# A two-layer trunk kernel: attention slots dealt out by ScalarE and VectorE load, evictions and splits queued in a given order, gated states of the recurrence copied a slot later

## The chip, the cores and the metric

The kernel runs on one core of a Trainium2 chip. A core has TensorE (PE in the profile; its weight loads are PEld), VectorE (DVE), ScalarE (ACT), GpSimd (POOL) and SyncE (SP), which here issues the loads and stores. The metric is the device time of one execution in microseconds (us), the median of several.

## The reference

One sequence of 1024 positions, width 1024, all float32:

```python
# layer 0: two groups of 8 heads of 64
proj = h @ w_in                      # a_q, a_k, a_v, b_q, b_k, b_v, f_logit, gate
# A: window of 128, 2 key/value heads, learned bias and a sink per head
# B: causal, logits + F_t - F_s, F = cumsum(log_sigmoid(f_logit + b_f))
y = concat(a_out, b_out) * silu(gate)
x = x + gate(c) * (y @ w_out)
# layer 1: recurrent block
xr, gate = split(h @ w_in)
xc = conv4(xr)                       # causal, depthwise
r, i = sigmoid(xc @ w_a + b_a), sigmoid(xc @ w_x + b_x)   # in 8 diagonal blocks
hs_t = a_t * hs_(t-1) + sqrt(1 - a_t^2) * (i * xc)_t,  a = exp(-8 softplus(lam) r)
x = x + gate(c) * ((hs * silu(gate)) @ w_out)
# RMSNorm with a scale and a shift that depend on c before each mixer; a last RMSNorm
```

## The kernel before, in words

The state lies transposed, width on the 128 partitions in 8 tiles, positions along the free axis in two halves of 512. A float32 operand is split in two parts: a rounded high part (names ending in hi or h), and the difference, the low part (lo, l). A product is then three matmuls: high x high, low weight x high, high weight x low. Writing the high part is a copy on ScalarE, the low part a subtraction on VectorE or GpSimd that needs the copy. Weights come from HBM into one of three `raw` buffers (256 KB each) and are split there, in two halves of four 128-row blocks, into `whi` and `wlo` (four buffers each). All instructions pass through helpers, so every row of the profile shows line 85, and the tiles' names tell the place.

By time in the profile: up to 133 us the modulation, the first norm and the gate projection; 133 to 530 attention, interleaved with the projections of q, k and v and the first part of the output projection; to 590 the rest of that projection (`o0c`) and the first tiles of the recurrent block's input projection (`lx`); to 780 the recurrence; then the last output projection (`ps_o`), in three column blocks, and the last norm.

**Attention.** A unit is one head (B) or one pair (A) and a pair j of 128-query blocks. It has steps: S (scores into `sA`/`sB`, added to the bias by VectorE, exponential on ScalarE into `pA`/`pB`), T (`turn`: transpositions of the probabilities on TensorE into `ptA`/`ptB`, then `split_t` into `pth` and `ptl`), V (`product`: `oA`/`oB` from `pth`, then from `ptl`) and E (`rbT`, the scaling of the result). For B with j = 3 there are four key-block pairs, `ptB_<head>_3_0` to `_3_3`. A slot holds the steps of neighbouring units that are issued together. `weave` walks through the slots and puts projection matmuls (`ps_fill`) between the steps; they come from the generator `fill`, job by job, and `weave` gives each slot as many as level its PE cost with the others'. A job ends with its eviction (`use_q`, `use_k`, `use_v`, for the output projection `residual` and `split_act`), at once after the last matmul. The next job's weights are loaded and split when a job starts. `drip` holds a few further copies, one per eight fill matmuls, `late` one more, the transposition of v.

TensorE's order in attention is that of the program, since `pe` is in the set `ordered`. The other engines' instructions are placed by the scheduler, by its own times; `paced(name)` adds an engine to the set for some instructions. In the start and the recurrence every engine is in program order.

**Recurrence.** `slot(c)` works on one tile c of eight: 24 matmuls for each half of the input tile c + 2 (`ps_lx`), the gates (`psr`, `psi`), 24 for each half of the gate path (`ps_lg`). ScalarE takes r_r and i_r (sigmoids), then tanh, exp, square and root; VectorE runs the convolution and the scan `hs`. The gated state is made in three steps: `gate_s` (sigmoid of `ps_lg` on ScalarE and the product on VectorE), `gate_a` (times `hs`, on GpSimd), `gate_b` (copy to y1h on ScalarE, y1l on GpSimd). `split_next` splits the next weights in line and loads the ones after. `last_slot` (c = 7) also splits the first tiles of the last output projection with `split_out`; `AHEAD` of these tiles run seven of their eight blocks before TensorE needs the last state.

Of the kernel before, what the change touches and what calls it, by code (L numbers as in the profile page):

```python
# [22 lines left out]
AHEAD = 3  # L23
# [25 lines left out]
def hybrid_trunk(  # L49
# [635 lines left out]
    def use_q(q, name):  # L685


        def use(h, ps):
            o = slice(h * HALF, (h + 1) * HALF)
            for hd, (a, b) in enumerate(((0, 64), (64, 0))):  # L690
                copy(q[hd][a : a + 64, o], ps[a : a + 64], scale=-0.125)
                dve.scalar_tensor_tensor(
                    out=q[hd][b : b + 64, o], in0=ps[a : a + 64], scalar=-0.125,
                    in1=r32(q[hd][a : a + 64, o]), op0=ALU.mult, op1=ALU.subtract,
                )

        return use

    def use_k(kh, kl):
        def use(h, ps):  # L700
            o = slice(h * HALF, (h + 1) * HALF)
            for hd, (a, b) in enumerate(((0, 64), (64, 0))):
# [7 lines left out]
                gp.tensor_copy(kl[hd][b : b + 64, o], r32(lo))  # L710

# [51 lines left out]
    def unit_a(p, j, q, kh, kl, out):  # L763
# [65 lines left out]
        def end():  # L829
# [4 lines left out]
            "S": [(0.43, lambda r=r: score(r)) for r in two],  # L834
            "T": [(0.43, lambda r=r: turn(r)) for r in two],
            "V": [(0.43, lambda r=r: product(r)) for r in two],
            "E": [(0.22, end)],
# [10 lines left out]
    def unit_b(p, hd, j, src, out):  # L848
# [61 lines left out]
        def end():  # L910
            finish(out()[0], box["rb"], 4 + p, j, f"B_{p}_{j}")

        return {
            "S": [
                (2 * max(b - a, 128) / 2400, lambda r=r, i=i: score(r, i))
                for r in range(2) for i, (a, b, _) in enumerate(pieces(2 * j + r))
            ],
            "T": [(0.43, lambda m=m: turn(m)) for m in range(j + 1)],
            "V": [(0.43, lambda m=m: product(m)) for m in range(j + 1)],
            "E": [(0.22, end)] if hd else [],  # L920
# [3 lines left out]
    def use_v(v, name):  # L924
        def use(h, ps):
            t = at.tile([P, HALF], F32, tag="tv", name=f"vt_{name}_{h}", bufs=1)
            copy(t, ps)

            def later():
                pt = ps_t(f"vT_{name}_{h}")  # L930
                for i in range(4):
                    tp(pt[:, i * P : (i + 1) * P], t[:, i * P : (i + 1) * P])
                for hd in range(2):
                    src = pt.rearrange("p (t h d) -> p t h d", t=4, h=2)[:, :, hd]
                    o = v[:, 4 * h : 4 * h + 4, hd]
                    copy(o[:, :, 0:64], src)
                    sub(dve, o[:, :, 64:128], src, r32(o[:, :, 0:64]))

            return later
# [5 lines left out]
    late, drip = [], collections.deque()  # L945

    def fill(jobs, ahead=lambda: None):

        jobs = list(jobs)
        ws = {0: jobs[0][0]()}  # L950
        for n, (_, ks, xs, use) in enumerate(jobs):
            if n + 1 < len(jobs):
                ws[n + 1] = jobs[n + 1][0]()
            else:
                ahead()
            w = ws.pop(n)
# [31 lines left out]
    def job(ti, name, use):  # L988
        return (lazy(lambda: load_tile(wt[ti], name)), range(KT), both, use)
# [70 lines left out]
    def weave(slots, gen, total, first=0):  # L1060


        cost = [sum(c for c, _ in s) for s in slots]
        left = total - sum(next(gen) for _ in range(first))
        for i, slot in enumerate(slots):
            rest = sorted(cost[i:])

            level, acc = 0.0, 0.0
            for n, c in enumerate(rest):
                level = (left + acc + c) / (n + 1)  # L1070
                acc += c
                if n + 1 == len(rest) or level <= rest[n + 1]:
                    break
            give = max(level - cost[i], 0.0)
            left -= give
            part = give / max(len(slot), 1)
            for _, f in slot:
# [17 lines left out]

    for n, _ in enumerate(fill(jobs[0], jobs[1][0][0])):
# [29 lines left out]
    def then_split(jq, jv, jk):  # L1126
# [4 lines left out]
        def use_and_split(h, ps):  # L1131
            use(h, ps)
# [533 lines left out]
```

## Time and profile before

| what | value |
|---|---|
| median of 3 executions | 888.19 us (884.86 to 888.86) |
| profiled execution | 888.44 us, span 886.7 us, granted clock 0.986 |
| PE busy | 860.7 us (97%) |
| DVE, ACT, POOL busy | 564.5 (64%), 535.7 (60%), 378.1 us (43%) |
| attention, 133 to 530 us | PE 388.93 of 397.00 us |
| a slot of the recurrence | 25.5 to 25.9 us, PE 24.95 to 25.90 us |

A PE duration runs until the modelled end of a matmul, and consecutive matmuls overlap in it; the distance from start to start tells the pace. In brackets behind a row stands the idle time of its engine before it and what ended it. A row of waits says which engine's work waited for which other, the sum, how often, and the longest. A row of a window gives its length and then the busy time of each engine in it.

### The profile page before, as it was taken

The page shows a single profiled execution, that of the slowest core. Times are in us where ns is not written, and L with a number is a line of the kernel's source. Part 1 is how long each engine was busy: PE and PEld are TensorE (multiplying, and loading weights), DVE is VectorE, ACT ScalarE, POOL GpSimd, SP SyncE. Part 2 cuts the span into 40 slices and gives each one's busy share as a digit, 9 for nine tenths or more (in the row PEclk, how much of TensorE's full clock was granted, in tenths as well). Part 3 has the DMA queues.
Part 4 walks back from the last instruction along what each step waited for, and adds up shares of the span by engine and source line. Part 5 has one row for each costly group of instructions (what it writes and reads, how often), then busy time and mean ns, then how long its engine had stood idle before and what let it go on. Part 6 is the DMA issues. An engine that isn't in the chain of part 4 may idle for free.

```text
span 886.7 us, 13483 instructions
## 1 busy us (share of the span) xinstructions
PE 860.7 (97%) x4618; PEld 730.7 (82%) x4618; DVE 564.5 (64%) x1136; ACT 535.7 (60%) x1047; POOL 378.1 (43%) x427
## 2 busy tenths in 40 slices
PE   9999999999989999999999999999899999999995
PEld 8887898888878888888777888878688877878995
DVE  7886657688676565565656668276556666583453
ACT  5765124788676666566656647358666667774432
POOL 4843322343342232331744656532565555475100
PEclk9999999999999999999999999999899999999998
DMA  9944772100013322322373564421212212126042
GB/s 344 404 185 127 216 229 60 49 25 20 30 53 111 107 80 101 123 87 78 110 240 104 184 209 145 145 79 44 78 54 72 77 57 67 56 71 226 7 149 83
DMA packets 54620, 103.83 MB, mean 117 GB/s; under 512 B 6960, under 2 KB 20720, under 8 KB 54040
## 3 DMA queue, kind: packets, MB, share of 16 engines
q1 hardware_dynamic: 53400, 101.93, 34.8%
q10 hardware_dynamic: 1152, 1.05, 0.5%
q8 instruction: 36, 0.59, 0.3%
q14 instruction: 32, 0.26, 0.1%
HBM read 94.02 MB, written 8.93 MB: 116 GB/s over the span
## 4 chain that ended last, share of the span: by engine, by line
PE 66%; ACT 11%; DVE 10%; DMA 5%; POOL 4%; issue 3%; SPq 0%; DVEq 0%; POOLq 0%; ACTq 0%
PE ps_fill L85 22%; PE ps_o L85 10%; PE pst L85 5%; PE ps_o0c L85 5%; PE oB L85 4%; PE sB L85 4%; PE ptB L85 3%; DVE xc_r L85 3%; PE ps_v L85 3%; DVE hs_r L85 2%; DMA ada<-in_ada_dram 2%; PE ps_lx L85 2%; POOL sg_r L85 2%; PE sA L85 2%; PE ps_lg L85 2%
## 5 line engine op out<-in xcount | busy, mean ns | idle before, releaser
L85 PE MATMUL ps_o<-y1h,wo 128*128 128x256 f32 (+1 forms) x336 | 76.8, 323 | 2.2 <-DVE wo L85 1.1
L85 DVE TENSOR_TENSOR ptl_B<-ptB,pth_B 128x512 fp32r<-128x512 f32 (+1 forms) x80 | 50.8, 636 | 36.8 <-ACT pth_B L85 36.3
L85 ACT ACTIVATE pth_B<-ptB 128x512 fp32r<-128x512 f32 (+1 forms) x80 | 44.0, 551 | 44.6 <-PE ptB L85 43.7
L85 ACT ACTIVATE pB<-pB,mnB 128x128 f32<-128x128 f32 (+3 forms) x64 | 49.5, 774 | 31.3 <-DVE mnB L85 25.9
L85 PEld LDWEIGHTS ps_o<-y1h,wo 128*128 128x128 f32 x336 | 56.7, 192 | 7.5 <-ACT wo L85 1.5
L85 POOL TENSOR_SCALAR_AFFINE_SELECT pB<-pB 128x128 f32<-128x128 f32 x64 | 18.8, 296 | 96.3 <-DMA pB<-gd 71.6
L85 PE MATMUL pst<-hh,ws 128*128 128x512 f32 x192 | 55.3, 396 | 0.1
L85 PE MATMUL ps_o<-y1l,wo 128*128 128x256 f32 (+1 forms) x168 | 54.2, 323 | 0.0
L85 PE MATMUL ps_lg<-h1h,wlo_lg 128*128 128x512 f32 x128 | 51.3, 401 | 2.3 <-POOL wlo_lg L85 2.3
L85 PE MATMUL ps_lg<-h1h,whi_lg 128*128 128x512 f32 x128 | 51.4, 401 | 1.9 <-ACT whi_lg L85 1.9
L85 DVE SCALAR_TENSOR_TENSOR xc_r<-ps_lx,col,xc_r 128x509 f32<-128x509 f32 (+2 forms) x48 | 35.7, 745 | 24.6 <-ACT xt_r L85 23.5
L85 PE MATMUL ps_lg<-h1l,whi_lg 128*128 128x512 f32 x128 | 50.8, 397 | 0.0
L85 PE MATMUL ps_lx<-h1l,whi_lx 128*128 128x512 f32 x128 | 50.3, 393 | 0.2 <-POOL h1l L85 0.2
L85 PE MATMUL ps_lx<-h1h,whi_lx 128*128 128x512 f32 x128 | 50.3, 393 | 0.0
L85 PE MATMUL ps_lx<-h1h,wlo_lx 128*128 128x512 f32 x128 | 50.1, 391 | 0.0
L85 DVE CUSTOM_DVE_ANT_0 pB<-sB,pB 128x384 f32<-128x384 f32 (+2 forms) x64 | 35.4, 554 | 19.4 <-PE sB L85 9.3
L85 ACT ACT_TABLE_LOAD x35 | 44.9, 1283 | 3.6 <-issue 1.9
L85 PE MATMUL ptB<-ident,pB 128*128 128x128 f32 x288 | 45.1, 273 | 1.2 <-DVE ptl_B L85 0.7
L85 PEld LDWEIGHTS ptB<-ident,pB 128*128 128x128 f32 x288 | 35.8, 140 | 12.2 <-PE rbT_B L85 1.5
L85 POOL TENSOR_TENSOR wlo_lx<-raw_lx,whi_lx 128x512 fp32r<-128x512 f32 x16 | 30.6, 1929 | 32.0 <-ACT whi_lx L85 30.1
L85 PEld LDWEIGHTS pst<-hh,ws 128*128 128x128 f32 x192 | 35.9, 188 | 9.0 <-DVE mod L85 0.6
L85 ACT ACTIVATE sq_o<-x 128x512 f32<-128x512 f32 (+1 forms) x33 | 18.0, 545 | 33.3 <-DVE x L85 33.1
(313 smaller groups left out, 2838.7 us busy)
## 6 DMA issues: line engine op xcount, KB each, us to landing
ada<-in_ada_dram SPq DMA_DIRECT2D x32, 512.0 KB
x<-in_xT_dram SPq DMA_DIRECT2D x20, 256.0 KB
ada<-in_ada_dram SPq DMA_DIRECT2D x4, 1024.0 KB
pB<-gd SPq DMA_DIRECT2D x8, 512.0 KB
raw_o0a<-in_wo_dram SPq DMA_DIRECT2D x16, 256.0 KB
raw_o0c<-in_wo_dram SPq DMA_DIRECT2D x16, 256.0 KB
x1d<-x SPq DMA_DIRECT2D x16, 256.0 KB
raw_lx<-in_wl_dram SPq DMA_DIRECT2D x16, 256.0 KB
```

The source lines that it names most:

```text
L85: ins = issue(*args, **kw)
```

## The change

- In attention, `split_t` keeps its two instructions in program order on ScalarE and VectorE. Evictions are no longer issued at the end of a job, but as a list of pieces put at the front of `drip`; one piece is taken every four fill matmuls, in program order on both engines. What is left is issued at the end of a `fill`. `late` is gone; the transposition and split of v are pieces of it too.
- Weights are objects: their loads go out at the start of the job before, their two splits are pieces of `drip`. The loads of `o0c_0` go out after the last `weave` instead of at the start of its last job.
- `weave` has three costs for a step, of PE, ScalarE and VectorE, and deals the fill so that a slot's PE time is in proportion to the larger of its two other loads.
- In the recurrence the y1h and y1l copies of tile c - 1 come in slot c, behind the tanh; the split of the gate weights stands directly behind i_r, also in slot 0, where it stood ahead of r_r. The rows for the modulation are loaded one slot ahead instead of two.
- In the last slot the splits of the output weights come earlier, all subtractions on GpSimd (the first tile's were on VectorE), and `AHEAD` goes from 3 to 4.

TensorE, around the end of head 4's unit j = 3 (`ptB_4_3_2` is the transposition of key-block pair 2, `oB` from `pth_B_4_3_2` and `ptl_B_4_3_2` its products). Before:

```order
L85 MATMUL ptB_4_3_2_4830<-ident_75,pB_4_7_4708 128x128
L85 MATMUL ps_fill_0_4728<-hlo_0_109,whi_bk_3_1_4613 128x512
L85 MATMUL ps_fill_0_4728<-hh_0_108,whi_bk_3_1_4613 128x512
L85 MATMUL oB_4_3_4823<-pth_B_4_3_1_4799,vb2_3960 128x256 x2
L85 MATMUL oB_4_3_4823<-ptl_B_4_3_1_4800,vb2_3960 128x256 x2
L85 MATMUL ps_fill_0_4728<-hh_0_108,wlo_bk_3_1_4614 128x512
L85 MATMUL ps_fill_0_4728<-hlo_0_109,whi_bk_3_1_4613 128x512
L85 MATMUL ptB_4_3_3_4847<-ident_75,pB_4_6_4666 128x128
L85 MATMUL ptB_4_3_3_4847<-ident_75,pB_4_7_4708 128x128 x2
L85 MATMUL ps_fill_1_4867<-hh_1_513,whi_bk_3_0_4607 128x512
L85 MATMUL ps_fill_1_4867<-hh_1_513,wlo_bk_3_0_4608 128x512
L85 MATMUL oB_4_3_4823<-pth_B_4_3_2_4835,vb2_3960 128x256 x2
```

The same place in the changed kernel:

```order
L85 MATMUL ptB_4_3_2_4831<-ident_75,pB_4_7_4708 128x128
L85 MATMUL oB_4_3_4825<-pth_B_4_3_1_4802,vb2_3955 128x256 x2
L85 MATMUL oB_4_3_4825<-ptl_B_4_3_1_4803,vb2_3955 128x256 x2
L85 MATMUL ptB_4_3_3_4844<-ident_75,pB_4_6_4653 128x128
L85 MATMUL ptB_4_3_3_4844<-ident_75,pB_4_7_4708 128x128 x2
L85 MATMUL ps_fill_0_4722<-hh_0_108,whi_bk_3_1_4691 128x512
L85 MATMUL oB_4_3_4825<-pth_B_4_3_2_4836,vb2_3955 128x256 x2
L85 MATMUL oB_4_3_4825<-ptl_B_4_3_2_4837,vb2_3955 128x256 x2
```

Between the last transposition of pair 2 and its first product stood six fill matmuls, now stands one.

ScalarE in slot 4 of the recurrence, from the sigmoid of tile 3's second half on. Before (a_r and then whi_lg_4 follow behind the last row):

```order
L85 ACTIVATE y1h_6672<-sg_r3_0_7572 128x512
L85 ACTIVATE sg_r3_1_7622<-ps_lg_3_1_7581 128x512
L85 ACTIVATE r_r4_7626<-psr_4_0_7606,col_85 128x512
L85 ACTIVATE r_r4_7626<-psr_4_1_7607,col_85 128x512
L85 ACTIVATE i_r4_7627<-psi_4_0_7614,col_85 128x512
L85 ACTIVATE i_r4_7627<-psi_4_1_7615,col_85 128x512
L85 ACTIVATE th_r4_7632<-r_r4_7626,sp_1267 128x1024
L85 ACTIVATE xch_r5_7637<-xc_r5_7490 128x1024
L85 ACTIVATE wrh_r5_7444<-wr_r5_7442 128x128
L85 ACTIVATE wrh_r5_7448<-wr_r5_7446 128x128
L85 ACTIVATE y1h_6672<-sg_r3_1_7622 128x512
L85 ACT_TABLE_LOAD
```

And changed:

```order
L85 ACTIVATE sg_r3_1_7618<-ps_lg_3_1_7577 128x512
L85 ACTIVATE r_r4_7621<-psr_4_0_7602,col_85 128x512
L85 ACTIVATE r_r4_7621<-psr_4_1_7603,col_85 128x512
L85 ACTIVATE i_r4_7622<-psi_4_0_7610,col_85 128x512
L85 ACTIVATE i_r4_7622<-psi_4_1_7611,col_85 128x512
L85 ACTIVATE whi_lg_4_0_7627<-raw_lg_4_0_7434 128x512
L85 ACTIVATE whi_lg_4_1_7633<-raw_lg_4_1_7537 128x512
L85 ACTIVATE th_r4_7639<-r_r4_7621,sp_1267 128x1024
L85 ACTIVATE y1h_6672<-sg_r3_0_7570 128x512
```

The copy of the gated state no longer stands ahead of r_r, and the high part of the gate weights stands behind i_r instead of behind a_r.

GpSimd in the last slot, from the first output tile's low parts on (`wo1_1_1` holds the low parts of tiles 1 to 4). Before:

```order
L85 TENSOR_TENSOR wlo_wo1_0_1_8206<-raw_wo1_0_1_8058,whi_wo1_0_1_8205 128x512
L85 TENSOR_TENSOR y1l_6673<-sg_r6_0_8097,y1h_6672 128x512
L85 TENSOR_TENSOR sg_r6_1_8211<-sg_r6_1_8211,hs_r6_8070 128x512
L85 TENSOR_TENSOR y1l_6673<-sg_r6_1_8211,y1h_6672 128x512
L85 TENSOR_TENSOR wo1_1_1_8232<-raw_wo1_2_0_8209,wo1_1_0_8231 128x512
```

And changed:

```order
L85 TENSOR_TENSOR wlo_wo1_0_1_8206<-raw_wo1_0_1_8037,whi_wo1_0_1_8205 128x512
L85 TENSOR_TENSOR y1l_6673<-sg_r6_0_8095,y1h_6672 128x512
L85 TENSOR_TENSOR wo1_1_1_8217<-raw_wo1_1_0_8043,wo1_1_0_8216 128x512
L85 TENSOR_TENSOR wo1_1_1_8217<-raw_wo1_1_1_8203,wo1_1_0_8216 128x512
L85 TENSOR_TENSOR wo1_1_1_8217<-raw_wo1_2_0_8209,wo1_1_0_8216 128x512
L85 TENSOR_TENSOR wo1_1_1_8217<-raw_wo1_2_1_8220,wo1_1_0_8216 128x512
L85 TENSOR_TENSOR sg_r6_1_8211<-sg_r6_1_8211,hs_r6_8068 128x512
```

The subtractions of tile 1 come to GpSimd, and with those of tile 2 they stand ahead of the last step of tile 6's second half.

The diff, cut to its core:

```diff
-AHEAD = 3
+AHEAD = 4
...
-        copy(hi[:, :w], pt[:, :w])
-        sub(dve, lo[:, :w], pt[:, :w], r32(hi[:, :w]))
+        with paced("act"), paced("dve"):
+            copy(hi[:, :w], pt[:, :w])
+            sub(dve, lo[:, :w], pt[:, :w], r32(hi[:, :w]))
...
-            "T": [(0.43, lambda m=m: turn(m)) for m in range(j + 1)],
-            "V": [(0.43, lambda m=m: product(m)) for m in range(j + 1)],
-            "E": [(0.22, end)] if hd else [],
+            "T": [(0.43, 0.6, 0.7, lambda m=m: turn(m)) for m in range(j + 1)],
+            "V": [(0.48, 0.4 * (m == j), 0.4 * (m == j), lambda m=m: product(m)) for m in range(j + 1)],
+            "E": [(0.22, 0.0, 0.4, end)] if hd else [],
...
+    EVERY = 4
+
+    def drop():
+        f = drip.popleft()
+        if f:
+            with paced("act"), paced("dve"):
+                f()
+
+    class Weights:
+        def __init__(self, src, name):
+            self.src, self.name, self.w = src, name, []
+
+        def load(self):
+            if self.w:
+                return []
+            raw = load_raw(self.src, self.name)
+            return [None] + [lambda r=r: self.w.extend(half_of(r)) for r in raw]
...
-                        if late and cnt == 9:
-                            late.pop()()
-                        if drip and cnt % 8 == 0:
-                            drip.popleft()()
+                        if drip and cnt % EVERY == 2:
+                            drop()
                         yield MM
-                x = use(h, ps)
-                if x:
-                    late.append(x)
+                drip.extendleft(reversed(use(h, ps)))
+        while drip:
+            drop()
...
-        cost = [sum(c for c, _ in s) for s in slots]
+        cost = [sum(x[0] for x in s) for s in slots]
+        load = [max(sum(x[1] for x in s), sum(x[2] for x in s)) for s in slots]
...
-            give = max(level - cost[i], 0.0)
+            lo, hi = 0.0, 100.0
+            for _ in range(50):
+                mid = (lo + hi) / 2
+                more = sum(max(mid * w - c, 0.0) for c, w in zip(cost[i:], load[i:]))
+                lo, hi = (mid, hi) if more < left else (lo, mid)
+            give = min(max(lo * load[i] - cost[i], 0.0), left)
...
-    weave(slots[cuts[7] :], fill(o0, lambda: load_o0c(0)), total(o0))
+    weave(slots[cuts[7] :], fill(o0), total(o0))
+    load_o0c(0)
...
         ps = gates(c)
-        if c == 0:
-            split_next()
-        else:
+        if c:
             gate_s(c - 1, 1)
-            gate_a(c - 1, 1)
         r, i_ = sig_ri(c, ps)
+        split_next()
...
         mul(dve, i_, i_, xcs[c])
+        if c:
+            gate_a(c - 1, 1)
+            gate_b(c - 1, 0)
...
-        if c:
-            split_next()
...
-        if n < KT:
-            gate_b(c, 0)
         mod_late(c)
+        load_row(c + 1)
...
         gate_b(c - 1, 0)
+        split_out(1)
         th, a_, a2 = rt("th", c), rt("a", c), rt("a2", c)
...
-        split_out(1, dve)
+        split_out(2)
         act.activation(th, th, AF.Sqrt, bias=tiny)
```

More of the change, by code (lines that the diff above doesn't have):

```diff
@@ L701, in use, with head @@
             o = slice(h * HALF, (h + 1) * HALF)
[L702 removed]
+            def head(hd, a, b):
                 copy(kh[hd][a : a + 64, o], ps[a : a + 64])
@@ L939, in use, with head @@
-            return later
+            pt = []
+            def head(hd):
+                if not hd:
+                    pt.append(ps_t(f"vT_{name}_{h}"))
+                    for i in range(4):
+                        tp(pt[0][:, i * P : (i + 1) * P], t[:, i * P : (i + 1) * P])
+                src = pt[0].rearrange("p (t h d) -> p t h d", t=4, h=2)[:, :, hd]
+                o = v[:, 4 * h : 4 * h + 4, hd]
+                copy(o[:, :, 0:64], src)
+                sub(dve, o[:, :, 64:128], src, r32(o[:, :, 0:64]))
@@ L941, in use_v @@
+            return [lambda: copy(t, ps), None, lambda: head(0), lambda: head(1)]
         return use
     MM = 512 / 2400
-    late, drip = [], collections.deque()
-    def fill(jobs, ahead=lambda: None):
-        jobs = list(jobs)
[L950 to L953, printed above, removed]
-            else:
-                ahead()
-            w = ws.pop(n)
+    drip = collections.deque()
@@ new lines, in hybrid_trunk, with fill @@
+    EVERY = 4
[12 more added lines that the diff above has]
+            return [None] + [lambda r=r: self.w.extend(half_of(r)) for r in raw]
+    def fill(jobs, after=None):
+        jobs = list(jobs)
+        for n, (weights, ks, xs, use) in enumerate(jobs):
+            ahead = jobs[n + 1][0] if n + 1 < len(jobs) else after
+            if ahead:
+                drip.extend(ahead.load())
+            w = weights.w
@@ L988, in job @@
     def job(ti, name, use):
-        return (lazy(lambda: load_tile(wt[ti], name)), range(KT), both, use)
+        return (Weights(wt[ti], name), range(KT), both, use)
     kha = [t4("KH", f"kha_{i}", F32R) for i in range(2)]
@@ L1094, in total @@
         return sum(len(ks) * 3 * len(list(xs())) * MM for _, ks, xs, _ in js)
+    for f in jobs[0][0][0].load():
+        if f:
+            f()
     for n, _ in enumerate(fill(jobs[0], jobs[1][0][0])):
```

63 lines of the change are left out of this document (22 added, 41 removed).

## The prediction

> **What bounds the kernel now.** I read the page's busy times first, then busy time by stage, then what TensorE (PE) waits for in each stage, and last the timeline at those waits. The page:
>
> ```profile
> span 886.7 us, 13483 instructions
> PE 860.7 (97%) x4618; PEld 730.7 (82%) x4618; DVE 564.5 (64%) x1136; ACT 535.7 (60%) x1047; POOL 378.1 (43%) x427
> ```
>
> PE is busy for 860.7 of 886.7 us, so 26.0 us is the most that any reordering can win unless matmuls disappear, and none do: PE issues the same 4618 in both kernels. Busy time by stretch (window, its length, then each engine's busy time and instructions, granted clock, DMA share, GB/s):
>
> ```profile
> 133.00:530.00 397.00, 388.93 (x2242) 330.97 (x2241) 262.79 (x691) 260.62 (x608) 156.19 (x259) 1.00 0.31 97
> 655.00:680.50 25.50, 25.50 (x113) 21.02 (x112) 15.47 (x18) 17.16 (x26) 14.56 (x11) 1.00 0.21 62
> 706.40:732.20 25.80, 24.95 (x110) 20.21 (x109) 15.75 (x18) 17.46 (x26) 14.87 (x11) 1.00 0.22 67
> ```
>
> Attention (133 to 530) has 397.00 - 388.93 = 8.1 us without PE work. A slot of the recurrence has either none (655 to 680.5) or 0.85 us (706.4 to 732.2). So the kernel is bound by PE nearly everywhere, and ScalarE and VectorE (17 and 16 of 26 us in a slot) matter only where a single result comes late. The waits of PE name those places, first in attention, then between 590 and 790 (engine, what waits, for whom: total us, times, longest):
>
> ```profile
> PE oB L85 <- ACT pth_B L85: 1.9, 3, 1.4
> PE oB L85 <- DVE ptl_B L85: 1.4, 2, 1.1
> PE rbT_A L85 <- POOL gy L85: 1.2, 1, 1.2
> PE rbT_B L85 <- DVE ptl_B L85: 0.9, 1, 0.9
> PE ptB L85 <- DVE ptl_B L85: 0.7, 2, 0.5
> ```
>
> ```profile
> PE ps_lg L85 <- POOL wlo_lg L85: 2.3, 3, 0.8
> PE ps_lg L85 <- ACT whi_lg L85: 1.9, 1, 1.9
> PE ps_o L85 <- DVE wo L85: 1.1, 1, 1.1
> PE ps_o L85 <- ACT wo L85: 1.1, 1, 1.1
> ```
>
> Five rows of attention hold 6.1 us, four rows of the recurrence and its last slot 6.4 us. The change is aimed at both, so the two sums are worked out apart.
>
> **The recurrence's gate weights.** PE's timeline in the slot at 714 and ScalarE's and GpSimd's beside it (start, duration, work, [idle before and its releaser]):
>
> ```profile
> 714.22 0.39 PE L85 MATMUL ps_lx<-h1h,wlo_lx 128*128 128x512 f32 x1
> ...
> 714.67 0.46 PE L85 MATMUL ps_lg<-h1h,whi_lg 128*128 128x512 f32 x1
> 715.98 0.50 PE L85 MATMUL ps_lg<-h1h,wlo_lg 128*128 128x512 f32 x1 [0.85 <-POOL wlo_lg L85]
> ```
>
> ```profile
> 705.26 0.63 ACT L85 ACTIVATE y1h<-sg_r 128x512 fp32r<-128x512 f32 x1 [6.99 <-POOL sg_r L85]
> 706.27 1.26 ACT L85 ACTIVATE r_r<-psr,col 128x512 f32<-128x512 f32 x2
> 707.41 1.28 ACT L85 ACTIVATE i_r<-psi,col 128x512 f32<-128x512 f32 x2
> 713.96 1.13 ACT L85 ACTIVATE whi_lg<-raw_lg 128x512 fp32r<-128x512 f32 x2
> ```
>
> ```profile
> 714.65 2.53 POOL L85 TENSOR_TENSOR wlo_lg<-raw_lg,whi_lg 128x512 fp32r<-128x512 f32 x2 [0.70 <-ACT whi_lg L85]
> 721.75 4.54 POOL L85 TENSOR_TENSOR wlo_lx<-raw_lx,whi_lx 128x512 fp32r<-128x512 f32 x2 [4.56 <-ACT whi_lx L85]
> ```
>
> Matmuls start 0.225 us apart (714.22 to 714.67 for two); their durations overlap, so what a wait costs is read from starts. From 714.67 to 715.98 is 1.31, so 1.1 us is lost. The chain: ScalarE sits idle 6.99 us for GpSimd's gated state, copies it (y1h), and only then takes the gates r_r (706.27); the split of the gate weights whi_lg comes at 713.96, after everything else; GpSimd's low half follows at 714.65. The 48 input matmuls (ps_lx) ahead of ps_lg start at 714.67 - 48 x 0.225 = 703.9, so the gates' sums were there 2.4 us before ScalarE took them up. The change does two things to this queue: y1h of the slot before moves behind the tanh, and whi_lg moves to directly behind i_r. With T for the end of the gates' matmuls, 703.9, r_r starts near T, whi_lg at T + 2.3 (1.14 from r_r to i_r, twice), wlo_lg 0.7 behind it as now, and that ends between T + 5.5 (2.53 for two) and T + 7.5 (4.54, the slowest pair above). PE needs it at T + 10.8. So this wait is gone with 3.3 to 5.3 us to spare. What is queued behind the moved pieces: tanh, 1.1 us behind whi_lg, but 1.3 us ahead in all, since r_r starts 2.4 earlier; the y1h copies land in ScalarE's idle time and are read only by the output projection. The row loads that now go out one slot later have a whole slot, 25.8 us.
>
> The same at the other places, from starts:
>
> ```profile
> 634.83 0.39 PE L85 MATMUL ps_lx<-h1l,whi_lx 128*128 128x512 f32 x1
> 637.11 0.75 PE L85 MATMUL ps_lg<-h1h,whi_lg 128*128 128x512 f32 x1 [1.89 <-ACT whi_lg L85]
> 638.45 0.80 PE L85 MATMUL ps_lg<-h1h,wlo_lg 128*128 128x512 f32 x1 [0.59 <-POOL wlo_lg L85]
> 639.05 0.63 PE L85 MATMUL ps_lg<-h1l,whi_lg 128*128 128x512 f32 x1
> 740.47 0.51 PE L85 MATMUL ps_lg<-h1h,whi_lg 128*128 128x512 f32 x1
> 741.82 0.50 PE L85 MATMUL ps_lg<-h1h,wlo_lg 128*128 128x512 f32 x1 [0.84 <-POOL wlo_lg L85]
> ```
>
> Slot 1: 639.05 - 634.83 - 3 x 0.225 = 3.5 us. Slot at 740: 1.35 - 0.23 = 1.1 us. With 714: 3.5 + 1.1 + 1.1 = 5.7 us, all by the same late whi_lg. In slot 0 the split is moved the other way, from ahead of r_r to behind i_r, and this is the one new risk here: I take it as just in time, with 0 to 1.5 us to lose.
>
> **The last slot.** There the first output weights are late:
>
> ```profile
> 784.53 0.39 PE L85 MATMUL ps_o<-y1l,whi_wo 128*128 128x512 f32 x1
> 786.00 0.49 PE L85 MATMUL ps_o<-y1h,wo 128*128 128x512 f32 x1 [1.08 <-ACT wo L85]
> 787.59 0.79 PE L85 MATMUL ps_o<-y1h,wo 128*128 128x512 f32 x1 [1.10 <-DVE wo L85]
> 788.18 0.63 PE L85 MATMUL ps_o<-y1l,wo 128*128 128x512 f32 x1
> ```
>
> 788.18 - 784.53 - 3 x 0.225 = 3.0 us. The change puts wo_1's copies ahead of the tanh on ScalarE instead of behind Exp and Square, its subtractions on GpSimd, and gives PE 84 matmuls of ps_o (63 before) ahead of the first that needs the last state: 21 x 0.225 = 4.7 us more cover, which the scan and its gate steps need, since the tanh now stands behind a copy that waits for its load. The gain is at most 3.0, and I take 2.5. Sum of recurrence and last slot: 5.7 + 2.5, less 0.2 for slot 0, is 8.0 us; bounds 4 and 8.7.
>
> The Trainium skill, "SBUF — State Buffer", summary of rules, says that when VectorE has two inputs in SBUF while GpSimd reads SBUF, the later of them waits until the other is done. The two wlo_lx subtractions above, 4.54 us beside VectorE's scan against 2.53 for wlo_lg, agree with it, though no row names the port. By it, as an estimate, each subtraction moved to GpSimd takes (4.54 - 2.53) / 2 = 1.0 us more, wo_1 comes that much later, and the sum would be 7.0 instead of 8.0.
>
> **Attention.** The split of the transposed probabilities (pth on ScalarE, then ptl on VectorE) now keeps its program order with the evictions, which come one piece per four fill matmuls. Copies of gated states (yh) in a bunch ahead of pth_B made the longest wait on it, 1.4 us:
>
> ```profile
> 422.56 1.13 ACT L85 ACTIVATE yh<-gy 128x512 fp32r<-128x512 f32 x2
> 423.61 0.84 ACT L85 ACTIVATE pth_B<-ptB 128x384 fp32r<-128x384 f32 x2
> ```
>
> Spread out, one piece in 4 x 0.225 = 0.9 us of fill, they leave pth at most one copy to wait for. I take 5.6 of the 6.1 us as gone. But fill is now dealt by the ScalarE and VectorE load of a slot, and the last units of a head lose theirs. The distance that matters, in the trace (a 512- and a 384-wide split, unhindered):
>
> ```profile
> 484.37 0.60 PE L85 MATMUL ptB<-ident,pB 128*128 128x128 f32 x4
> 485.07 0.60 ACT L85 ACTIVATE pth_B<-ptB 128x512 fp32r<-128x512 f32 x1 [0.96 <-PE ptB L85]
> 485.70 0.69 DVE L85 TENSOR_TENSOR ptl_B<-ptB,pth_B 128x512 fp32r<-128x512 f32 x1 [1.39 <-ACT pth_B L85]
> 485.98 0.49 PE L85 MATMUL ptB<-ident,pB 128*128 128x128 f32 x3
> 487.00 0.40 PE L85 MATMUL oB<-ptl_B,vb 128*128 128x256 f32 x2
> ```
>
> A transposition takes 0.60 - 0.49 = 0.11, four of them 0.44, so the first tile is whole at 484.81; its low half is there at 485.70 + 0.69 = 486.39, 1.58 us later, and PE comes for it at 487.00. In the new order (shown above for head 4, j = 3), between the last transposition of block 2 and its low products stand four products of 256 columns, three transpositions, one fill and the two high products: 6 x 0.113 (half of 0.225 each) + 3 x 0.11 + 0.225 = 1.23 us. So 0.35 us is missing, in each of the eight units with j = 3: 2.8 us at least. A dripped piece of some 0.6 us can stand ahead on either engine; with half a piece the price is (0.35 + 0.3) x 8 = 5 us, with one on each engine (0.35 + 0.6 + 0.69) x 8 = 13 us. Block 3 follows in the shadow of that wait. I take 5, nearer to the lower end, because there is a single fill, so at most one piece, in that distance. Attention then is -5.6 + 5 = -0.6; bounds -3.3 and +13, and -6.1 where only the old waits count. The loads of o0c_0 now leave only after the last weave. GpSimd still has their subtractions ahead of the last gate row's copy, with PE's last attention products beside them, so I cost that at nothing, and at one pair of subtractions, 2.5 us, if this cover is gone.
>
> **Sum.** The profiled execution took 888.44 us, 1.7 more than its span and 0.25 more than the median. 888.4 - 8.0 - 0.6 = 879.8, say 880 us.
>
> **Rivals.**
> Attention keeps its gain: the dripped pieces fall into idle time (ScalarE 260.62 of 397 us) and the close products find slack that the count above has not seen; 888.4 - 8.7 - 6.1 = 873.6 us. For it speaks that both engines are below 70% there; against it that order, not load, made every wait shown.
> The recurrence gives half: slot 0's whi_lg comes 1.5 us late, and in the last slot wo_1's second half still waits for its load, whose buffer GpSimd frees no earlier than before, so that 3.0 stay: 888.4 - 5.7 + 1.5 - 0.6 = 883.6, say 884 us. Against it: the three middle waits have one cause and nothing new in front.
> Slower: one mechanism, the close products of block 2 at j = 3. If a dripped copy (0.6) and a subtraction (0.69) stand in order ahead of pth and ptl in each of the eight units, attention costs 13 and wins nothing back, since the old waits only move: 888.4 - 8.0 + 13 = 893 us. It decides from (0.35 + x) x 8 = 8.0 + 5.6 on, x = 1.35 us of queue per unit where the old waits go, and 0.65 where they stay. Against it: pieces are issued only at fills, and the single fill there lets one through.
> The change does nothing measurable: slots bound by the 113 PE instructions (25.50 of 25.50 us) and the waits reappear one step on; 887 us.
>
> **How the numbers follow.** Forecast 0.52, attention's gain kept 0.15, half a recurrence 0.13, slower 0.12, nothing 0.08. 0.5% is 4.4 us, what can be told here from no change: faster is below 883.8. Of the forecast 0.46 lies below that and 0.06 above, of the half 0.06 and 0.07. That gives faster 0.46 + 0.15 + 0.06 = 0.67, no change 0.06 + 0.07 + 0.08 + 0.01 = 0.22, and slower 0.11. Range: below, 872 takes in the gain kept; above, 888 takes in the half and nothing; outside stay the slower case and a few hundredths below. The forecast's own range is 876 to 884.
>
> **What would show it.** Right: no wait of ps_lg on wlo_lg or whi_lg from slot 1 on, r_r within 0.3 us of the last gate matmul, ScalarE's wait for sg_r no longer ahead of r_r; ps_o with at most 0.5 us on wo; slots of 24.7 to 25.7 us. In attention: no wait over 1 us on pth_B, and new waits of 0.3 to 0.8 us of oB on ptl_B, at the last blocks of j = 3. Wrong: attention longer than 397 us by more than 4, or a ps_lg wait in slot 0 over 1.5 us, or ps_o still waiting for wo.

## The result, and the profile after

The changed kernel takes 910.28 us (median of four executions, 906.97 to 912.25) against 887.75 us; the ratio is 1.0255, with a 95% interval of 1.0216 to 1.0295. It is slower by 22.5 us. The forecast of 880 us was on the wrong side. Its profiled execution took 909.7 us; the page:

```profile
span 907.9 us, 13468 instructions
PE 864.9 (95%) x4618; PEld 731.2 (81%) x4618; DVE 563.6 (62%) x1134; ACT 539.5 (59%) x1047; POOL 386.5 (43%) x429
```

PE's work has not grown in count (4618). Of the 21.2 us that the span is longer, 17.0 are idle time of PE (26.0 us before, 43.0 now) and 4.2 are busy time. Busy time by stretch, cut where a stage's first matmul starts: attention, then the recurrence with its first input tiles, then the last projection. First the kernel before, then the changed one:

```profile
133.00:521.00 388.00, 379.93 (x2203) 323.68 (x2202) 255.01 (x680) 255.66 (x600) 152.20 (x256) 1.00 0.30 95
571.50:780.00 208.50, 203.73 (x887) 165.91 (x885) 130.06 (x157) 140.82 (x206) 108.28 (x76) 0.98 0.21 66
780.00:882.00 102.00, 95.31 (x605) 86.22 (x603) 52.16 (x93) 45.71 (x79) 30.30 (x22) 0.97 0.32 106
```

```profile
133.00:550.00 417.00, 388.54 (x2205) 326.83 (x2205) 255.28 (x679) 257.55 (x600) 151.81 (x255) 0.99 0.27 87
600.50:804.50 204.00, 201.43 (x886) 165.35 (x885) 132.24 (x157) 141.08 (x204) 116.03 (x77) 0.99 0.21 69
804.50:903.00 98.50, 93.42 (x605) 85.15 (x604) 47.89 (x89) 46.83 (x80) 30.89 (x23) 1.00 0.31 107
```

Attention went from 388.0 to 417.0 us: 29 us longer, with almost the same number of instructions on every engine. PE's idle time there grew by 20.4 us (8.1 to 28.5) and its busy time by 8.6. Part of the 8.6 is a slower clock: in three stretches of 3.4 us (from 154.8, 349.4 and 468.9), each at the end of one of the long waits below or up to 1.4 us behind it, the granted clock is 0.50; before, there was one such stretch (from 425.6). Two more of them at half speed are, as an estimate, 3.4 us of matmul time lost. The recurrence is 4.5 us shorter, and the last projection, to the end of each span (886.7 and 907.9 us), 3.3; 29.0 - 4.5 - 3.3 = 21.2. So the two halves of the change did opposite things, and attention decides. The waits of PE there (engine, what waits, for whom: total, times, longest), which were five rows with 6.1 us before, and three small ones with 1.4:

```profile
PE ptB L85 <- ACT pB L85: 7.5, 6, 2.5
PE oB L85 <- DVE ptl_B L85: 4.2, 9, 1.4
PE ps_fill L85 <- DVE kla L85: 4.2, 1, 4.2
PE ptB L85 <- DVE ptl_B L85: 2.8, 3, 1.3
PE ptA L85 <- DVE gy L85: 2.3, 3, 0.8
PE ps_fill L85 <- POOL wlo_o0a L85: 2.1, 2, 1.7
PE ptA L85 <- DVE ptl_A L85: 2.0, 4, 1.0
PE vT_bv L85 <- ACT vt_bv L85: 1.9, 1, 1.9
```

Eight rows hold 27.0 us. Only the second was expected, as a wait of 0.3 to 0.8 us in eight places. There are three main kinds: probabilities that come too late (pB, ptl), evictions that come too late (kla, vt), and a split of weights that comes too late (wlo_o0a). Behind attention, two waits stand where four were:

```profile
PE psr L85 <- POOL wrl_r L85: 2.0, 1, 2.0
PE ps_o L85 <- POOL wo L85: 0.8, 1, 0.8
```

No row of ps_lg on wlo_lg or whi_lg is left.

### The profile page after: what moved, and what is told of

It reads as the page before. It is cut to its first block, busy times and chain, and to the rows that moved or that the text cites. A ratio compares the mean times of both kernels' runs of the same rounds, so it can differ in the third digit from the quotient of the medians.

```text
span 907.9 us, 13468 instructions
## 1 busy us (share of the span) xinstructions
PE 864.9 (95%) x4618; PEld 731.2 (81%) x4618; DVE 563.6 (62%) x1134; ACT 539.5 (59%) x1047; POOL 386.5 (43%) x429
## 5 line engine op out<-in xcount | busy, mean ns | idle before, releaser
L85 PE MATMUL ptB<-ident,pB 128*128 128x128 f32 x288 | 47.6, 278 | 11.1 <-ACT pB L85 7.5
L85 POOL TENSOR_TENSOR wlo_lg<-raw_lg,whi_lg 128x512 fp32r<-128x512 f32 x16 | 34.6, 2184 | 16.1 <-issue 9.7
```

The lines of the kernel that those rows point to most:

```text
L85: ins = issue(*args, **kw)
```

## The experiments

The change has four parts that can be put in singly: the recurrence's edits (with the last slot and `AHEAD`), the dealing of fill by load, the queue of evictions and splits, and the program order of `split_t`. All kernels below have the recurrence's edits; the parts of attention are added one by one.

### The recurrence's edits alone

```diff
 (attention as before)
-AHEAD = 3
+AHEAD = 4
 (slot and last_slot as in the change)
```

> Only the recurrence and last-slot edits (and AHEAD 4); attention as before. Theory 'attention alone lost the time': 880 us (888 less the 7.7 us that the two later stretches are shorter in the changed kernel's trace), slots of 25 to 26 us, no wait of ps_lg on wlo_lg, and the new wait of psr on wrl_r (2 us) there too, since it comes from the moved copies. Rival 'the recurrence gains only because attention ended in another state': 886 to 888 us.

Measured: 879.74 us against 886.93; ratio 0.9924 (0.9900 to 0.9948). The recurrence's part of the forecast holds alone. The new wait of 2 us on wrl_r is here too, so it belongs to these edits. This kernel, 879.7 us, is the base of the runs that follow.

### The dealing of fill alone

```diff
-        cost = [sum(c for c, _ in s) for s in slots]
+        cost = [sum(x[0] for x in s) for s in slots]
+        load = [max(sum(x[1] for x in s), sum(x[2] for x in s)) for s in slots]
 (and the rest of weave; queue and split_t as before)
```

> Recurrence edits, and of the attention edits only the dealing of fill by ScalarE and VectorE load; evictions, weight splits and split_t as before. Theory D (the dealing makes the waits: biased scores pB and the split ptl come too late for TensorE): 880 + 18 = 898 us, with the waits of ptB on pB (7 us) and of oB and ptB on ptl_B (7 us) all there. Theory Q (the queue of evictions makes them): 880 to 884 us, and those two rows at the 1 to 3 us of the kernel before.

Measured: 891.31 us, 11.6 over the base; ratio to the kernel before 1.0038 (1.0023 to 1.0052). ptB waits 5.4 us for pB, but oB and ptB only 2.9 us for ptl_B. So theory D holds in kind for pB but hardly for ptl_B, with about two thirds of its size (11.6 of 18). A single wait of 2.0 us of rbT_B on wlo_o0a is here too. The longest of the waits on pB, in the timeline of this kernel, every engine's rows in order of time (start, duration, work, idle before):

```profile
274.25 0.39 PE L85 MATMUL sB<-klb,bq 128*128 128x512 f32 x1
...
275.26 0.29 POOL L85 TENSOR_SCALAR_AFFINE_SELECT pB<-pB 128x128 f32<-128x128 f32 x1 [0.68 <-DMA pB<-gd]
275.52 0.73 POOL L85 TENSOR_TENSOR gy<-gy,y_A 128x256 f32<-128x256 f32 x1
...
276.28 0.42 DVE L85 TENSOR_TENSOR y_B<-oB,tmp 64x256 f32<-64x256 f32 x1 [2.57 <-POOL gy L85]
276.62 0.67 DVE L85 CUSTOM_DVE_ANT_0 pB<-sB,pB 128x512 f32<-128x512 f32 x1
...
277.40 0.72 ACT L85 ACTIVATE pB<-pB,mnB 128x512 f32<-128x512 f32 x1 [1.89 <-DVE mnB L85]
...
278.27 0.55 PE L85 MATMUL ptB<-ident,pB 128*128 128x128 f32 x3 [2.25 <-ACT pB L85]
```

The scores are complete at 274.6. VectorE is idle for 2.57 us, but the first in its queue is y_B, which waits for GpSimd's gy; that stands behind a mask, and the mask waits for the load of pB's bias. Only then come the biased scores, the exponential and the transposition. In five of the seven places the exponential is 512 wide, the fourth query block of a head (j = 1); in the other two it is 1024 wide. For that block two distances, counted in the order of TensorE's instructions at the trace's pace, have shrunk in the changed kernel: from its scores to its first transposition, 2.05 to 2.7 us before, now 1.4 to 1.6 us in every other head and 2.0 to 2.7 in the rest; and from the last transposition of the head before (which frees the bias buffer) to the end of those scores, 5.0 to 5.9 us before, now 4.1 to 4.6.

### Without GpSimd's gy in that chain

```diff
-        mul(gp, g, g, y[:, 2 * j : 2 * j + 2].rearrange("p a b -> p (a b)"))
+        mul(dve, g, g, y[:, 2 * j : 2 * j + 2].rearrange("p a b -> p (a b)"))
```

> The dealing alone (recurrence edits too), and the last product of a unit's gated result (gy) moved from GpSimd to VectorE, so that nothing stands on GpSimd between a masked bias that waits for its load and VectorE's y_B. Theory 'chain': the load of pB's bias holds GpSimd's mask, GpSimd's gy behind it holds VectorE's y_B, and y_B stands ahead of the biased scores that TensorE's ptB needs: waits of ptB on pB fall from 5.4 to under 1.5 us, time 891.3 - 4 = 887. Rival 'TensorE is simply too close behind its scores': the waits stay at 5 us, time 890 to 894 with VectorE's added 0.4 us a unit.

Measured: 890.23 us; ratio 1.0034 (1.0019 to 1.0050). The theory of the chain falls: the waits on pB are 5.6 us in eight places, the longest 1.5 instead of 2.2. The chain is real where it stands, but when its middle link is taken out, the load itself is the last link:

```profile
400.63 0.30 POOL L85 TENSOR_SCALAR_AFFINE_SELECT pB<-pB 128x128 f32<-128x128 f32 x1 [2.04 <-DMA pB<-gd]
...
401.08 0.67 DVE L85 CUSTOM_DVE_ANT_0 pB<-sB,pB 128x512 f32<-128x512 f32 x1
...
402.66 0.55 PE L85 MATMUL ptB<-ident,pB 128*128 128x128 f32 x3 [1.46 <-ACT pB L85]
```

So the rival is left: TensorE is too close, and whichever link is last, the time from the freed buffer to the transposition no longer holds load, mask, scores, exponential.

### Light slots given more

In the weave, a product is due two slots behind its transposition, and scores, loads and buffers follow by slots as well. Levelled by PE cost, each slot in the middle of attention lasted 1.77 us (PE cost plus fill, in the planner's own figures). Dealt by load, a slot of one transposition and one product, of a load of 0.7, lasts 0.91 + 0.15 = 1.06 us, and three of these follow one another. So a distance that was counted in slots shrank. Here no load counts for less than 1.2:

```diff
-        load = [max(sum(x[1] for x in s), sum(x[2] for x in s)) for s in slots]
+        load = [max(1.2, sum(x[1] for x in s), sum(x[2] for x in s)) for s in slots]
```

> As the run with the dealing alone, but no slot's load counts for less than 1.2, so that a light slot (one transposition, one product) is dealt 1.6 us of TensorE work instead of 1.06; levelled by TensorE cost it was 1.77. Theory 'distance counted in slots': a product stands two slots behind its transposition and the biased scores a fixed number of slots behind their load, so short light slots are what brings TensorE too early: the waits on pB and ptl fall from 8 to under 3 us and the time to 881 to 884 (879.7 without any dealing, 891.3 with it). Rival 'the heavy slots' longer stretches or the engines' order lose it': 888 to 891 as before.

Measured: 880.46 us; ratio 0.9931 (0.9912 to 0.9950). All of the dealing's 11.6 us but 0.7 are gone, and the longest rows of PE's waits in attention are:

```profile
PE oB L85 <- ACT pth_B L85: 1.9, 1, 1.9
PE ptB L85 <- ACT pB L85: 1.2, 4, 0.6
PE oB L85 <- DVE ptl_B L85: 0.9, 4, 0.3
```

One number in the planner, with nothing else changed, takes the loss away. From the scores of the fourth query block to its first transposition it is 2.0 to 2.3 us again in every head, while from the freed buffer to these scores it is still only 4.1 to 5.0. So the dealing costs its time through short distances, which come from the light slots. The rival of the heavy slots is not wholly apart from this, since the floor also shortens the longest slot, from 2.96 to 2.57 us in the planner's figures. The dealing also wins nothing over the base, 879.7.

### The queue and split_t's order, without the dealing

```diff
+    EVERY = 4
 (drop, Weights, the lists of pieces, split_t with paced)
 (weave and its costs as before)
```

> Recurrence edits, and of the attention edits all but the dealing: evictions and weight splits as pieces in a given order, split_t in program order, fill levelled by TensorE cost as before. Theory D: 880 + 8 = 888 us, with only the waits of evictions and weights (kla 4.2, vt 1.9, wlo_o0a 2). Theory Q: 900 to 908 us, waits on pB and ptl as in the changed kernel.

Measured: 896.65 us, 16.9 over the base; ratio 1.0103 (1.0086 to 1.0119). This lies between the two theories. Of the 30.5 us by which the changed kernel lies above the base, 13.6 come with the dealing and 16.9 with the queue and the order. The waits on pB are nearly gone (1.2 us against 7.5), those on ptl mostly stay (7.4 against 9.2).

### The same, with the decay sums later

The wait of 4.2 us on kla, in the changed kernel. VectorE:

```profile
148.94 3.25 DVE L85 TENSOR_SCALAR loc<-loc 8x256 f32<-8x256 f32 x6
152.22 0.68 DVE L85 TENSOR_TENSOR kla<-ps_fill,kha 64x512 fp32r<-64x512 f32 x1
```

and PE:

```profile
150.46 0.39 PE L85 MATMUL ps_fill<-hlo,whi_aq 128*128 128x512 f32 x1
155.00 0.76 PE L85 MATMUL ps_fill<-hh,whi_aq 128*128 128x512 f32 x1 [4.15 <-DVE kla L85]
```

The eviction of the second half of k became two pieces, so its subtractions are issued a few matmuls after the sums of the forget gate (`decay`) instead of ahead of them, and VectorE works these off first. PE needs the bank and stands still.

```diff
-        if n == 48:
+        if n == 58:
             decay()
```

> As the run with the queue and paced split_t but without the dealing, and VectorE's decay sums issued ten fill matmuls later, behind both queued evictions of that tile. If the 4.2 us wait of ps_fill on kla is only the eviction standing behind those sums: it is gone, 896.6 - 4.3 = 892.3. If the eviction is late by itself: a wait on kla of 2 us or more stays and the time is above 894.

Measured: 890.30 us; ratio 1.0041 (1.0024 to 1.0058). No wait on kla is left, and the time fell by 6.4 us, 2 more than that wait. The cause of the wait is shown, and the trace without the later sums shows what followed from it. PE's windows there, behind the wait, which ends at 154.74 in that kernel:

```profile
154.74:159.50 4.76, 4.76 (x11) 3.77 (x12) 1.68 (x3) 1.48 (x3) 3.33 (x3) 0.50 0.20 59
159.50:166.60 7.10, 7.10 (x33) 5.82 (x31) 1.38 (x2) 3.09 (x5) 1.21 (x1) 1.00 0.11 35
```

The granted clock is 0.50 up to 159.50 and 1.00 after it. The 11 matmuls of the first window start 0.43 us apart, those of the second 0.23: 11 x 0.20 = 2.2 us lost on top of the wait. With the sums later, the clock is 1.00 from 145 to 160.

### The changed kernel without split_t's order, and the queue alone

```diff
-        with paced("act"), paced("dve"):
-            copy(hi[:, :w], pt[:, :w])
-            sub(dve, lo[:, :w], pt[:, :w], r32(hi[:, :w]))
+        copy(hi[:, :w], pt[:, :w])
+        sub(dve, lo[:, :w], pt[:, :w], r32(hi[:, :w]))
```

> The changed kernel with split_t's copy and subtraction again placed by the scheduler; all else as changed. If the given order of split_t blocks ScalarE and VectorE (heads of line): 900 us or less, waits on ptl halved. If it does not matter: 908 to 912 us. If it helps: over 915 us.

Measured: 900.73 us; ratio 1.0148 (1.0130 to 1.0166), 9.6 us less than the changed kernel. So the order costs 9.6 there, about what the first theory gave (900 or less); but the waits on ptl (6.2 against 9.2 us) did not halve.

> Recurrence edits and the queue of evictions and weight splits, without the dealing and with split_t placed by the scheduler. If the given order of split_t costs 9 us wherever it stands (as between the changed kernel and the one without it): 896.6 - 9 = 888. If it costs only together with the dealing: 895 to 897. The waits of ptA on gy (3.2 us) go with it in the first case.

This kernel has the queue and neither of the other parts. Measured: 890.70 us; ratio 1.0039 (1.0021 to 1.0057). This lies between the two guesses. The queue alone costs 11.0 us, the order on top of it 6. Beside the known wait of 4.1 us on kla there is one of 3.3 us, the longest in its largest row of waits (ptB on ptl_B, 5.3 us in all). GpSimd, VectorE and PE:

```profile
458.74 0.60 POOL L85 TENSOR_SCALAR_AFFINE_SELECT pB<-pB 128x128 f32<-128x128 f32 x2 [4.01 <-DMA pB<-gd]
459.06 0.29 DVE L85 CUSTOM_DVE_ANT_0 pB<-sB,pB 128x128 f32<-128x128 f32 x1 [2.66 <-POOL pB L85]
459.28 0.69 DVE L85 TENSOR_TENSOR ptl_B<-ptB,pth_B 128x512 fp32r<-128x512 f32 x1
...
460.11 0.63 PE L85 MATMUL ptB<-ident,pB 128*128 128x128 f32 x4 [3.33 <-DVE ptl_B L85]
```

GpSimd's mask waits for the load of the bias, the biased scores behind it stand ahead of ptl in VectorE's queue, and PE waits for ptl. The 4.0 us in which GpSimd was idle do not tell how late the load was: in the base GpSimd waits up to 7.9 us for such a load. In this kernel the weights' loads go out a job ahead, on the same SyncE queue as the bias; whether one held up the other was not tried by itself.

### The queue with evictions at once

```diff
-                drip.extendleft(reversed(use(h, ps)))
+                todo = use(h, ps)
+                if len(todo) < 3:
+                    for f in todo:
+                        f()
+                else:
+                    drip.extendleft(reversed(todo))
```

Only weights' splits, and the copy and transposition of v, are still pieces.

> As the run with the queue alone (890.7), but the evictions of q, k and the output projection are issued at once at the end of a job, as before the change; only weight splits and the copy and transposition of v stay queued. Theory 'late evictions': the wait of ps_fill on kla (4.1) and the last job's waits on wlo_o0a (2.5, its split was crowded out of the queue) go, time 884. Rival 'weights split late': the waits on wlo_o0a and of ptB on ptl_B (5.3) stay, time 886 to 888.

Measured: 882.02 us; ratio 0.9945 (0.9930 to 0.9960). 8.7 of the queue's 11.0 us go with the evictions issued at once; the wait on kla is 0.9 us, none on wlo_o0a is left, and ptB waits 1.9 us for ptl_B instead of 5.3. The rival, that the weights' splits are late by themselves, falls: they were crowded out by the evictions.

### split_t's order alone

```diff
+        with paced("act"), paced("dve"):
+            copy(hi[:, :w], pt[:, :w])
+            sub(dve, lo[:, :w], pt[:, :w], r32(hi[:, :w]))
 (queue and weave as before)
```

> Recurrence edits, and of the attention edits only the program order of split_t's copy and subtraction. If that order costs by itself what it cost beside the queue (6 us) and beside queue and dealing (9.5): 885 to 889, with waits of ptA on gy and ptl_A. If it costs only because queued pieces share the order: 879 to 881, no wait of more than 1 us that was not there before.

Measured: 891.11 us, 11.4 over the base and more than either guess; ratio 1.0056 (1.0040 to 1.0071). The order costs by itself, without any queued piece. TensorE issues in the same order in this kernel as in the base, matmul by matmul, so each delay can be read as a lag. The largest, 2.7 us, is the first of these rows of this kernel's waits,

```profile
PE oA L85 <- DVE ptl_A L85: 2.7, 1, 2.7
PE oB L85 <- DVE ptl_B L85: 2.9, 8, 0.8
```

where VectorE worked off an eviction, a cast and two biased scores that came earlier in the program, and then ptl. In the base the scheduler had put ptl ahead of these (VectorE in the base):

```profile
255.59 0.68 DVE L85 TENSOR_TENSOR ptl_A<-ptA,pth_A 128x512 fp32r<-128x512 f32 x1
256.63 0.69 DVE L85 TENSOR_TENSOR klb<-ps_fill,khb 64x512 fp32r<-64x512 f32 x1 [0.37 <-ACT khb L85]
```

The same loss in the changed kernel, ScalarE, VectorE and PE in order of time:

```profile
329.60 1.19 ACT L85 ACTIVATE khb<-ps_fill 64x512 fp32r<-64x512 f32 x2 [0.88 <-DVE klb L85]
...
330.81 0.49 ACT L85 ACTIVATE pth_B<-ptB 128x384 fp32r<-128x384 f32 x1
...
331.44 0.69 DVE L85 TENSOR_TENSOR klb<-ps_fill,khb 64x512 fp32r<-64x512 f32 x1
...
332.16 0.42 DVE L85 CAST khb<-khb 64x512 fp32r<-64x512 f32 x1
...
332.62 0.56 DVE L85 TENSOR_TENSOR ptl_B<-ptB,pth_B 128x384 fp32r<-128x384 f32 x1
...
333.23 0.45 PE L85 MATMUL oB<-ptl_B,vb 128*128 128x256 f32 x2 [1.37 <-DVE ptl_B L85]
```

pth_B is written by 331.30, but ptl_B starts at 332.62, behind an eviction (0.69) and a cast (0.42) for which PE does not wait here.

### The wait on wrl_r, first try

In the recurrence's last slot but one, without input matmuls, the next gates come early. GpSimd had the copies of the gated state ahead of the split of their weights.

```diff
-        if c:
+        if 0 < c < KT - 2:
             gate_a(c - 1, 1)
             gate_b(c - 1, 0)
         split_xc(c + 1)
         split_r(c + 1)
+        if c == KT - 2:
+            gate_a(c - 1, 1)
+            gate_b(c - 1, 0)
```

> Recurrence edits alone, and in the last slot but one the next tile's gate weights (wrl) are split ahead of the copies of the gated states. If the wait of psr on wrl_r (2.2 us) is only that order on GpSimd: it is gone, 879.7 - 2.2 = 877.5. If GpSimd is late by itself there (its low gate weights took 4.5 us beside VectorE): 1 us or more of it stays, 879 us.

Measured: 881.81 us; ratio 0.9944 (0.9925 to 0.9963): nothing gained. The wait on wrl_r is gone, and beside the three attention kernels that ran on the same chip (recurrence 202.3 us, last projection up to PE's last matmul 98.0) the recurrence is 2.1 us shorter, but the last projection 3.0 us longer:

```profile
PE ps_o L85 <- POOL wo L85: 2.8, 2, 1.7
PE ps_o L85 <- POOL wlo_wo L85: 1.8, 1, 1.8
```

And ScalarE in that slot:

```profile
759.72 0.63 ACT L85 ACTIVATE y1h<-sg_r 128x512 fp32r<-128x512 f32 x1 [5.92 <-POOL sg_r L85]
```

A copy that nobody needs yet waits 5.9 us for GpSimd, and the exponential, the scan and the last weights' split stand behind it.

### The wait on wrl_r, second try

```diff
         split_r(c + 1)
-        if c == KT - 2:
-            gate_a(c - 1, 1)
-            gate_b(c - 1, 0)
...
         act.activation(th, th, AF.Sqrt, bias=tiny)
+        if c == KT - 2:
+            gate_a(c - 1, 1)
+            gate_b(c - 1, 0)
+            gate_b(c - 1, 1)
```

> Recurrence edits alone, and in the last slot but one the next gate weights (wrl) are split first and the copies of the gated states stand behind the square root, so that ScalarE's exp does not wait behind them (5.9 us idle ahead of y1h in the run with wrl split first). If the wait moved on to wlo_wo only because ScalarE and with it the scan stood behind those copies: rec and last projection together 200 + 97, time 875 to 877.5, no wait on wrl_r or wlo_wo over 0.5 us. If GpSimd's own queue is the limit there: 880 to 882 as in that run.

Measured: 876.15 us against 886.15; ratio 0.9885 (0.9869 to 0.9902). Of the waits of psr and ps_o these are left:

```profile
PE psr L85 <- POOL wrl_r L85: 0.5, 1, 0.5
PE ps_o L85 <- POOL wo L85: 0.2, 1, 0.2
```

This is the fastest kernel of the study, 10 us below the one before and 34 below the changed one: the recurrence's edits of the change, one slot mended, and attention left alone.

## Why the prediction was wrong

The parts of attention, each over the base of 879.7 us: dealing 11.6, queue 11.0, split_t's order 11.4. Their sum, 34.0, is near the 30.5 us by which the changed kernel lies above the base. Together they cost a little less than one by one: queue and order 16.9 us, not 22.4. So the forecast's sum, -8.0 and -0.6, should have been about -8 and +30.

- **"What bounds the kernel now"**: right that PE bounds it nearly everywhere and that only late single results matter. It follows that moving load evenly over ScalarE and VectorE can win nothing but the few waits, and can lose many.
- **"The recurrence's gate weights" and "The last slot"**: the mechanism is right, and the sum is near in part by luck. Forecast 5.5 and 2.5 us, together 8.0; measured by stretches 4.5 and 3.3, and 7.2 us by the times of the run with these edits alone. But two errors met. TensorE's order is the same in both traces up to the last projection, so the losses can be read as lags: the three late whi_lg cost 8.4 us, not 5.7, of which slot 1 had 5.9, not 3.5. The prediction counted slot 1 only up to the start at 639.05, but the matmuls go on at a distance of 0.43 us up to 644. The window of the kernel before shows a granted clock of 0.57:

```profile
636.00:644.00 8.00, 6.30 (x14) 4.64 (x15) 4.38 (x5) 6.71 (x10) 2.90 (x3) 0.57 0.27 79
```

Against that stands the wait of 2.0 us on wrl_r, the cost of the moved copies on GpSimd, which was not forecast; with the stretch at half clock around it (758.9 to 762.3) its lag is 3.8 us. With that slot mended, the gain is 10 us, as the last run shows. The estimate worked out from the rule of the Trainium skill, "SBUF — State Buffer", summary of rules, that a subtraction moved to GpSimd takes 1.0 us longer, did not hold for wo_1. GpSimd in the kernel with the recurrence's edits alone, and after it VectorE:

```profile
775.05 2.54 POOL L85 TENSOR_TENSOR wo<-raw_wo,wo 128x512 fp32r<-128x512 f32 x2
786.09 4.96 POOL L85 TENSOR_TENSOR wo<-raw_wo,wo 128x512 fp32r<-128x512 f32 x2
```

```profile
785.01 3.27 DVE L85 TENSOR_TENSOR_SCAN hs_r<-a_r,i_r 128x1024 f32<-128x1024 f32 x1
```

The first pair is wo_1, with VectorE idle for most of it: 2.54 us for two. The second pair, a later tile, ran beside the scan and took 4.96 us for two, which agrees with the rule.
- **"Attention then is -5.6 + 5 = -0.6; bounds -3.3 and +13"**: this is the step that failed, in three of its terms.
  - The term "5.6 of the 6.1 us as gone": saw in the program order of split_t, with the pieces spread out, only a gain, since it keeps bunches of copies out of the way. The order takes away the scheduler's freedom to put ptl ahead of work for which TensorE does not wait, and that costs 11.4 us alone. There was a row that pointed at it: before, ScalarE and VectorE were idle for a third of attention and PE had few waits, so the existing order was already good.
  - The term "0.35 us ... in each of the eight units with j = 3": the place was right, the size less than forecast. In the changed kernel the low products of block 2 wait 0.2 us each in seven of these eight units, 1.5 us in all where 5 were forecast; with the dealing alone it is the same, 1.4 us. But the count was made for one pair of rows, transposition to product. The same shortening acts on everything that is counted in slots, and with the dealing alone the larger part was on pB, from bias load and scores to transposition: 5.4 us, 4.7 of it at j = 1.
  - Evictions as queued pieces were priced at nothing but as pieces ahead of pth. What waits for them, the bank that the next tile needs and the weights' splits behind them in the same queue, was not asked. That was 8.7 us, most of it at one place, behind the decay sums: 6.4 us, wait and slow clock together, in the run that moved the sums.
- **The rivals**: the slower one, 893 us, had the right sign, but not the mechanism that decided; the changed kernel lies 17 us above it. Its condition, a copy and a subtraction ahead in each of the eight units with j = 3, was met in none of them: in the changed kernel oB waits 0.2 us for ptl_B in seven of the eight. Work does stand ahead of ptl_B, as in the rows around 332 above, but there and at 402 (1.4 us each) the unit is one with j = 2.
- **The range** ended at 888, although the text gave +13 as a bound of attention, which with -8 is 893. The bound itself was set by one mechanism.

Open stays why the queue with weights' splits alone still costs 2.3 us, and whether SyncE's order of loads made a bias late.

## What to carry to other kernels

When a schedule counts distances in slots, whatever sets the length of a slot sets these distances too: before changing how work is dealt, list every producer and consumer that is a fixed number of slots apart and find the shortest. A fixed order on an engine is a loss as soon as something that nobody waits for stands ahead of something that TensorE waits for. Deferring an eviction delays its reader by more than the deferral if other work is issued in between, and a bank, a buffer and a queue are readers too. A long wait of TensorE can cost more than its own length: look at the granted clock and at the distance of the starts behind it before a wait is priced.

## What the runs showed of the hardware that was not expected

Behind some long waits TensorE ran at half clock: 0.50 from 154.74 to 159.50 in the run with queue and order, behind a wait of 4.15 us, with starts 0.43 us apart instead of 0.23. In the changed kernel's attention such a stretch belongs to three waits, of 4.15, 2.45 and 1.86 us, but another wait of 2.48 us (418.6) has none; no run here shows what decides it.

VectorE's decay sums work on 8 partitions and at most 896 columns, little data, and still held the engine from 145.2 to 152.2 us; six of them took 3.25 us, 0.34 us with 256 columns to 0.68 with 896. A subtraction of 64x512 took 0.68 us there (kla) and one of 128x512 took 0.69 (ptl_B at 459.28): in these rows the time goes by the columns, and the number of partitions does not show. GpSimd's low halves of 512 columns took 2.5 us a pair alone and 4.5 to 5.0 us beside VectorE's scan or its products; a plan that counts 1.3 us each on GpSimd is off by a factor of nearly two there.
